# RWKV work given out anew over the 24 slots of a unit, with VectorE and ScalarE in emission order

## The chip, the cores and the metric

One core of a Trainium2 chip runs the kernel. The metric is the device time of one execution in microseconds (us). A core has a matrix engine (TensorE, PE in the profile, with its weight loads as PEld), VectorE (DVE), ScalarE (ACT), GpSimd (POOL) and SyncE (SP, which issues most DMAs).

## The reference, cut to what matters

A decoder layer on 1024 tokens of width 1024. After an RMSNorm, one projection feeds two branches whose outputs are concatenated, projected and normalised:

```python
p = einsum('bsd,dn->bsn', rms_norm(h, norm_w), w_in)     # 1024 x 8320 columns
y_rwkv = rwkv7_time_mix(p_shifted, gate, ...)            # 16 heads of 64
y_att = mixed_dilated_attention(p[..., ATT0:ATT_GATE0], p[..., ATT_GATE0:])
h = h + einsum('bsm,md->bsd', concatenate([y_rwkv, y_att]), w_out)
# inside rwkv7_time_mix, for each token t:
state = state * w_t + sa * b_t + v_t * k_t               # 64 x 64 per head
y_t = state @ r_t                                        # then group norm, bonus, gate
```

## The kernel before

All is float32. The RWKV recurrence is computed in chunks of 64 tokens. Two heads (a pair) and one half of the sequence (512 tokens, 8 chunks) make a *unit*; there are 16 units, `units[0..15]`. The loop over `p` from -2 to 15 in `rwkv` works on four units at once, in stages:

- `prepare` and `products` for unit p+2: norms of the keys (`norm`), decay rates (`decay`), running sums (`sums`), their exponentials, the removal keys and receptance, and 32 small matmuls per unit (`step`). `relayout` sends a triangular matrix through DRAM (`ld`) and `load` reads it back as `AB`.
- `late` and `invert` for unit p+1: transposes of keys and values, and a triangular inverse: 15 `column` steps on VectorE that read `AB` and write `UB`, then `back`, which sends `UB` through DRAM into `U`, then four matmul steps `m1` to `m4`.
- `chain` for unit p: the recurrence itself. Per chunk three steps (`first`, `second`, `third`); each is a few 128-column matmuls, then `spread`: one half of the result is copied by VectorE (zd, ud or Sd), the other by ScalarE, and the next step's matmul reads both. 8 chunks make 24 steps.
- `finish` for unit p-1: group norm (`norm`), transposes and gate (`store`), and the DMA to `mixd`.

Each pass over p has `NSLOT` = 24 slots. Slot s holds step s of the chain, and the other stages put their pieces into slots by number (constants `PREP`, `LATE`, `MS`, `FIN`, `COL0`, `BACK`, `LT`, `PROD`). After the pieces of a slot, `advance(4)` (in pass 13 `advance(2)`, before pass 0 `advance(5)`) emits *projection steps*: 512-column matmuls of the big input projection (`proj_steps`, L187), which have no tie to the chain. 24 of them make a half block; its last one is followed by `take` (one ScalarE and one VectorE pass over 128x512, `shift` or `gate`). A new weight block is fetched every 12 slots (`wload`: two ScalarE casts `wh` and two VectorE differences `wl`).

Emission order is not execution order. The framework's planner walks through the program once at build time with its own estimates of durations: each engine takes, among the instructions that are ready by that estimate, the one that was emitted first. Semaphores are added afterwards. On the chip each engine then follows that fixed order.

After the RWKV units come attention, which takes the remaining projection steps, and the output projection.

Of the kernel before, what the change touches and what calls it, by code (L numbers as in the profile page):

```python
# [20 lines left out]
HD = 64  # L21
# [3 lines left out]
C = 64  # L25
# [8 lines left out]
WARM = (4, 0)  # L34
V_AT = (-2, 3, -1)
COL0 = 0
COLN = 4
BACK = 9
LT = 12
MS = (16, 18, 20, 21)  # L40
LATE = (0, 3, 11, 10)
PREP = (2, 5, 6, 7, 8, 9, 10)
FIN = (1, 3, 7)
PROD = 10
# [9 lines left out]
class Kern:  # L54
# [237 lines left out]
    def rwkv(self, pairs=range(NPAIR), apairs=range(NPAIR)):  # L292
        nc = self.nc
        with ExitStack() as ctx:
# [49 lines left out]
            for p in range(-2, N):  # L344
                dA, dI, dC, dF = get(p + 2), get(p + 1), get(p), get(p - 1)
                ev = [[] for _ in range(NSLOT)]
                put = lambda steps: [ev[s].append(f) for s, f in steps]
                if dC:
                    put(enumerate(self.chain(dC, get(p + 1) if dC["h"] == 0 else None)))
                if dF:  # L350
                    put(self.finish(dF))
                if dI:
                    put(self.late(dI))
                    put(self.invert(dI, self.Us[(p + 1) % 2]))
                if dA:
                    lag = WARM[p + 2] if p < 0 else 0
                    put([(n + lag, f) for n, f in self.prepare(dA) + self.products(dA)])
                if get(p + 3) and get(p + 3)["h"] == 0:
                    ev[12].append(lambda d=get(p + 3): self.lora_w(d))
                elif get(p + 3):  # L360
                    get(p + 3)["lw"] = get(p + 2)["lw"]
                if p == -2:
                    px = self.prep_x(1, self.lng, tags, ba)
                    for s in range(4):
                        ev[s].append(lambda: [next(px, None) for _ in range(2)])
                    ev[4].append(lambda: [None for _ in px])
                n = 5 if p < 0 else 2 if dA is not None and get(p + 3) is None else 4
                for s in range(NSLOT):
                    for f in ev[s]:
                        f()  # L370
                    self.advance(n)
# [22 lines left out]
    def prepare(self, d):  # L394
# [8 lines left out]
        def decay():  # L403
# [6 lines left out]
            th = self.tmp("gt0", "th")  # L410
# [3 lines left out]
            lw = self.lw  # L414
# [4 lines left out]
        def sums(i):  # L419
# [6 lines left out]
            if i == 0:  # L426
                return
            I = d["I"]
            W = d["W"] = self.tmp("vr0", "W", L)
            S.activation(out=W, in_=I, func=AF.Exp, scale=-1.0)  # L430
            Ux = d["Ux"] = self.tmp("vr1", "Ux", L)
# [3 lines left out]
            S.copy(out=d["dec"][:, 1], in_=Ux[64:128, :, 0])  # L435

        def norm():
            sq = self.tmp("qr1", "sq")
            S.activation(out=sq, in_=d["ks"], func=AF.Square, scale=col(P_KK))
            sqt = self.ps_tr.tile([128, 4, 2, HD], F32, name="sqt", tag="tr")  # L440
            for b in range(4):
                nc.tensor.transpose(out=sqt[:, b].rearrange("p a b -> p (a b)"), in_=sq[:, b * 128:(b + 1) * 128],
                                    identity=self.ident)
            nq = self.mid.tile([128, 4, 2], F32, name="nq")
# [10 lines left out]
        def removal():  # L455
# [5 lines left out]
            V.scalar_tensor_tensor(out=b2, in0=c3(ta), scalar=1.0, in1=Ux[:, :, 1:C + 1], op0=ALU.add, op1=ALU.mult)  # L461
            V.scalar_tensor_tensor(out=b2, in0=c3(ks), scalar=col(P_KK), in1=b2, op0=ALU.mult, op1=ALU.mult)
            S.activation(out=ta, in_=ta, func=AF.Identity, scale=self.hka[:, pr:pr + 1], bias=self.oka[:, pr:pr + 1])
            V.tensor_tensor(out=ks, in0=ks, in1=ta, op=ALU.mult)
            V.tensor_tensor(out=BK[:, :, 64:128], in0=c3(ks), in1=Ux[:, :, 1:C + 1], op=ALU.mult)
# [10 lines left out]
        return list(zip(PREP, (norm, decay, lambda: sums(0), lambda: sums(1), removal, receptance, bonus_parts)))  # L476

    def late(self, d):
# [3 lines left out]
        pr = d["pr"]  # L482

        def values():
            vq = self.ps_tr.tile([128, 4, 2, HD], F32, name="vq", tag="tr")
            for b in range(4):
                nc.tensor.transpose(out=vq[:, b].rearrange("p a b -> p (a b)"), in_=d["vs"][:, b * 128:(b + 1) * 128],
                                    identity=self.ident)
            for par in range(2):
# [4 lines left out]
        def keys(c4):  # L494
            cs = slice(c4 * 4, c4 * 4 + 4)
            tq = self.ps_tr.tile([128, 4, 2, HD], F32, name="tq", tag="tr")
            for b in range(4):
                nc.tensor.transpose(out=tq[:, b].rearrange("p a b -> p (a b)"), in_=d["BK"][:, c4 * 4 + b],
                                    identity=self.ident)
            for e in range(2):  # L500
# [4 lines left out]
        def bonus():  # L505
            bq = self.ps_tr.tile([128, HALF], F32, name="bq", tag="tr")
            for i in range(2):
                nc.tensor.matmul(bq, lhsT=self.bdr, rhs=d["bs"][i], start=(i == 0), stop=(i == 1))
            d["bv"] = self.lng.tile([128, HALF], F32, name="bv", bufs=2)
            V.tensor_tensor(out=d["bv"], in0=bq, in1=d["vs"], op=ALU.mult)  # L510
        return list(zip(LATE, (lambda: keys(0), lambda: keys(1), values, bonus)))

    def products(self, d):
# [4 lines left out]
        def step(c4):  # L518
# [7 lines left out]
            for b in range(4):  # L526
                c = c4 * 4 + b
                for e in range(2):
                    nc.tensor.matmul(q[e][:, b], lhsT=BK[er[e], c], rhs=AR[er[e], c * 192 + 64:c * 192 + 192], start=True,  # L529
                                     stop=True)  # L530
            for e in (1, 0):
# [21 lines left out]
        steps = [(PROD + 2 * c4, lambda c4=c4: step(c4)) for c4 in range(2)]  # L553
        return steps + [(PROD + 5, relayout), (PROD + 5, load)]

    def invert(self, d, U):
# [33 lines left out]
        def m1():  # L590
# [3 lines left out]
            xq = self.ps_tr.tile([128, NC_, 16], F32, name="xq", tag="tr")  # L594
            for c in range(NC_):
                for g in range(4):
                    b = 32 * (g % 2)
                    nc.tensor.matmul(xq[hs(g), c], lhsT=t["LT"][rs(g), c, b:b + 16], rhs=U[rs(g), c, b + 16:b + 32], start=True,
                                     stop=True, skip_group_check=True)
            for g in range(4):  # L600
                S.copy(out=t["Xs"][hs(g), :, 0:16], in_=xq[hs(g)])
# [500 lines left out]
```

## Time and profile before

| what | value |
|---|---|
| median of three runs | 1561.51 us (1561.48 to 1563.06) |
| the profiled execution, its own time | 1562.53 us |
| its span in the trace | 1560.8 us |
| PE busy in the span | 1490.8 us (96%) |
| DVE busy | 1029.8 us (66%) |
| ACT busy | 891.8 us (57%) |
| mean granted TensorE clock | 0.997 of full |

The span is the trace from the first to the last instruction; the execution's own time has 1.7 us around it. The page's line of the clock shows full speed in all 40 slices. The chain of the first unit starts at about 118 us and that of the last ends at about 850 us. The chain of work that ended last is by engine PE 67%, DVE 18%, ACT 10%.

### The profile page before, as it was taken

To read this page: it belongs to the slowest core of one execution; us is meant where nothing else is said; L and a number is where in the kernel's file an instruction comes from. 1 tells how busy PE (TensorE), PEld (TensorE's weight loads), DVE (VectorE), ACT (ScalarE), POOL (GpSimd) and SP (SyncE) were. 2 spreads that over 40 slices of the span, in tenths; PEclk is the share of its full clock that TensorE was granted. 3 is DMA by queue.
4 is the path that set the end of the run, shared out by engine and by line. 5 is a ranking of instruction groups with operands and counts; after the bars stand their busy time and mean duration, and the time that the engine had idled before them with its cause. 6 is when DMAs were issued, how large, how long until landed. Compare 5 with 4: busy or idle time off the path is not lost.

```text
span 1560.8 us, 29095 instructions
## 1 busy us (share of the span) xinstructions
PE 1490.8 (96%) x10721; PEld 1211.8 (78%) x10721; DVE 1029.8 (66%) x2776; ACT 891.8 (57%) x2080; POOL 455.3 (29%) x563
## 2 busy tenths in 40 slices
PE   5999999999999999999999999999999999899997
PEld 4777777777777777777677788888888888787886
DVE  6867876777866768767644557666686676856144
ACT  6556666666666666665653556555565665645221
POOL 3122111121201212112111434333343344456442
PEclk9999999999999999999999999999999999999999
DMA  6221111111111111111111201111111111426452
GB/s 198 66 66 40 39 34 41 45 34 48 32 42 40 42 38 45 27 41 46 31 31 43 70 28 42 35 35 34 35 55 28 41 55 55 155 96 196 144 163 98
DMA packets 178829, 94.87 MB, mean 61 GB/s; under 512 B 58413, under 2 KB 164606, under 8 KB 178686
## 3 DMA queue, kind: packets, MB, share of 16 engines
q1 hardware_dynamic: 174942, 86.19, 19.4%
q10 hardware_dynamic: 3744, 6.82, 1.3%
q8 instruction: 84, 1.38, 0.4%
q14 instruction: 59, 0.48, 0.1%
HBM read 75.01 MB, written 17.83 MB: 59 GB/s over the span
## 4 chain that ended last, share of the span: by engine, by line
PE 67%; DVE 18%; ACT 10%; issue 3%; DMA 1%; POOL 1%; DVEq 0%; SPq 0%; POOLq 0%; ACTq 0%
PE pq L187 33%; PE oq L986 10%; PE T L645 4%; PE z L645 3%; PE o L932 3%; PE mp L859 2%; PE sp L892 2%; PE pa L529 2%; PE sp L912 1%; PE sp L911 1%; ACT zt L726 1%; DVE wl L179 1%; ACT MV L535 1%; PE x L621 1%; DVE I L424 1%
## 5 line engine op out<-in xcount | busy, mean ns | idle before, releaser
L187 PE MATMUL pq<-xh,wh 128*128 128x512 f32 x1040 | 428.9, 413 | 0.0
L187 PE MATMUL pq<-xl,wh 128*128 128x512 f32 x1040 | 416.4, 400 | 0.0
L187 PE MATMUL pq<-xh,wl 128*128 128x512 f32 x1040 | 294.8, 404 | 0.0
L187 PEld LDWEIGHTS pq<-xl,wh 128*128 128x128 f32 x1040 | 196.9, 189 | 32.0 <-DVE xl L166 0.2
L187 PEld LDWEIGHTS pq<-xh,wh 128*128 128x128 f32 x1040 | 196.5, 189 | 32.2 <-ACT xh L165 0.2
L187 PEld LDWEIGHTS pq<-xh,wl 128*128 128x128 f32 x1040 | 185.4, 189 | 31.9
L986 PE MATMUL oq<-ow,qr 128*128 128x512 f32 x512 | 161.9, 394 | 1.2 <-ACT ow L967 0.6
L920 POOL TENSOR_TENSOR pl<-p,ph 128x512 fp32r<-128x512 f32 (+2 forms) x96 | 102.2, 1071 | 202.5 <-ACT ph L919 182.3
L861 DVE CUSTOM_DVE_ANT_0 mp<-mp,maskq 128x512 f32<-128x512 f32 (+1 forms) x192 | 105.5, 570 | 67.6 <-PE mp L859 59.1
L915 ACT ACTIVATE p<-p 128x512 f32<-128x512 f32 (+2 forms) x144 | 64.6, 452 | 103.4 <-DVE p L914 102.5
L179 POOL TENSOR_TENSOR wl<-wraw,wh 128x512 fp32r<-128x512 f32 x64 | 85.2, 1351 | 110.5 <-ACT Sd L660 36.2
L981 POOL TENSOR_TENSOR vr<-kr,qr 128x512 fp32r<-128x512 f32 (+2 forms) x68 | 91.1, 1346 | 80.3 <-ACT qr L980 73.8
L986 PEld LDWEIGHTS oq<-ow,qr 128*128 128x128 f32 x512 | 95.9, 188 | 22.7 <-ACT ow L967 1.1
L986 PE MATMUL oq<-ow,vr 128*128 128x512 f32 x256 | 101.2, 395 | 2.0 <-POOL vr L981 2.0
L178 ACT CAST wh<-wraw 128x512 fp32r<-128x512 f32 x138 | 80.3, 618 | 39.2 <-PE pq L187 31.2
L980 ACT CAST qr<-kr 128x512 fp32r<-128x512 f32 (+2 forms) x68 | 40.1, 594 | 95.1 <-PE oq L986 49.8
L914 DVE TENSOR_TENSOR p<-sp,maskt 128x512 f32<-128x512 f32 (+2 forms) x144 | 65.2, 457 | 43.0 <-PE sp L912 41.5
L645 PEld LDWEIGHTS T<-ud,TU 128*128 128x128 f32 x256 | 40.8, 188 | 47.6 <-ACT ud L660 42.0
L660 ACT ACTIVATE Sd<-T,dec 64x64 f32<-64x64 f32 x120 | 36.9, 307 | 67.5 <-DVE Sd L659 66.2
L645 PE MATMUL T<-ud,TU 128*128 128x128 f32 x256 | 58.4, 310 | 16.8 <-ACT ud L660 15.6
L659 DVE TENSOR_SCALAR Sd<-T,dec 64x64 f32<-64x64 f32 x120 | 32.9, 274 | 60.4 <-PE T L645 58.2
L660 ACT ACTIVATE ud<-z,rn 64x64 f32<-64x64 f32 x128 | 39.3, 307 | 50.6 <-DVE ud L659 47.6
(236 smaller groups left out, 3173.5 us busy)
## 6 DMA issues: line engine op xcount, KB each, us to landing
wraw<-in_w_in_dram SPq DMA_DIRECT2D x138, 256.0 KB
kr<-mixd SPq DMA_DIRECT2D x60, 256.0 KB
oraw<-in_w_out_dram SPq DMA_DIRECT2D x16, 512.0 KB
xt<-in_x_dram SPq DMA_DIRECT2D x8, 512.0 KB
ld<-TU SPq DMA_DIRECT2D x32, 128.0 KB
mixd<-zt SPq DMA_DIRECT2D x16, 256.0 KB
mixd<-gt SPq DMA_DIRECT2D x16, 256.0 KB
xr<-in_x_dram ACTq DMA_DIRECT2D x16, 256.0 KB
```

The costliest lines, as they stand in the source:

```text
L178: nc.scalar.copy(out=wh[:, ks], in_=raw)
L179: eng.tensor_tensor(out=wl[:, ks], in0=raw, in1=wh[:, ks].bitcast(F32), op=ALU.subtract)
L187: return [lambda i=i, a=a, b=b: self.nc.tensor.matmul(q, lhsT=a, rhs=b, start=(i == 0), stop=(i == len(ops) - 1)) for i, (a, b) in enumera ...
L645: mm = lambda out, w, x, start, stop: nc.tensor.matmul(out, lhsT=w, rhs=f2(x), start=start, stop=stop, skip_group_check=True)
L660: S.activation(out=out[er[1], 1], in_=q[0:64, 64:128], func=AF.Copy, scale=scale[1])
L861: V.tensor_tensor_reduce(out=mp[:, :kn], in0=mp[:, :kn], in1=self.maskq[:, v0:v0 + kn], op0=ALU.add, op1=ALU.max, scale=1.0, scalar=-3e38, ...
L914: V.tensor_tensor(out=p[:, :qn], in0=sp[:, :qn], in1=self.maskt[:, u0:u0 + qn], op=ALU.add)
L915: S.activation(out=p[:, :qn], in_=p[:, :qn], func=AF.Exp)
L920: G.tensor_tensor(out=pl[:, :qn], in0=p[:, :qn], in1=ph[:, :qn].bitcast(F32), op=ALU.subtract)
L932: nc.tensor.matmul(oc, lhsT=v, rhs=w[:, :qn], start=(first and i == 0), stop=(last and i == len(prods) - 1), skip_group_check=True)
L981: nc.gpsimd.tensor_tensor(out=ml, in0=raw, in1=mh.bitcast(F32), op=ALU.subtract)
L986: nc.tensor.matmul(q, lhsT=m[:, i], rhs=v, start=(k == 0 and j == 0), stop=(k == 15 and j == 2))
```

## The change

Two things are changed, both inside `rwkv`. The loop over p now stands in a block in which the planner keeps VectorE and ScalarE in emission order; PE, GpSimd and SyncE are still placed by it. And the pieces are cut finer and put into other slots. Most pieces that had a matmul and the copy of its result in one slot now have the copy in the next slot.

| piece | slot before | slot after |
|---|---|---|
| keys transposes, halves 0 and 1 (PE / copies) | 0, 3 | 0 / 1, 2 / 3 |
| values (PE / copies), bonus (PE / product) | 11, 10 | 9 / 10, 11 / 12 |
| columns 0 to 14 | 0-3, four to a slot | 2,2,2,4,5,6,6,6,7,8,8,8,9,9,10 |
| back, lt | 9, 12 | 11, 12 |
| m1, m2, m3, m4 (PE) | 16, 18, 20, 21 | 16, 18, 21, 22 |
| their transposes and copies | same slots | 15; 17, 19 and 20, 22, 23 |
| key norms: square, PE, sums | 2 | 2, 4, 5 |
| decay: PE, tanh, log | 5 | 7, 8, 9 |
| running sums; W; Ux, dec, a | 6, 7; 7; 7 and 8 | 10, 11; 11; 12 |
| removal, receptance, bonus parts | 8, 9, 10 | 13-15, 16, 21 |
| products, two steps (PE / masks and copies) | 10, 12 | 17 / 18, 19 / 20 |
| relayout and load | 15 | 22 |
| finish: copy out, norm, store | 1, 3, 7 | 0; 1 to 4; 5 to 7 |
| lag of `prepare` in the first pass, `WARM` | 4 | 1 |

```diff
-            for p in range(-2, N):
+            with self.tc.manual_schedule(engines={mybir.EngineType.DVE, mybir.EngineType.Activation}):
+                for p in range(-2, N):
...
-        return list(zip(PREP, (norm, decay, lambda: sums(0), lambda: sums(1), removal, receptance, bonus_parts)))
+        return [(2, square), (4, squares), (5, norm), (7, decay), (8, rates), (9, logs), (10, lambda: sums(0)), (11, lambda: sums(1)),
+                (11, growth), (12, decrease), (13, removal), (14, removal2), (15, removal3), (16, receptance), (21, bonus_parts)]
...
-        return list(zip(LATE, (lambda: keys(0), lambda: keys(1), values, bonus)))
+        return [(0, lambda: keys(0)), (1, lambda: keys2(0)), (2, lambda: keys(1)), (3, lambda: keys2(1)), (9, values),
+                (10, values2), (11, bonus), (12, bonus2)]
...
-        steps = [(PROD + 2 * c4, lambda c4=c4: step(c4)) for c4 in range(2)]
-        return steps + [(PROD + 5, relayout), (PROD + 5, load)]
+        return [(17, lambda: step(0)), (18, lambda: step2(0)), (19, lambda: step(1)), (20, lambda: step2(1)), (22, relayout),
+                (22, load)]
...
+        return [(COLS[j], lambda j=j: column(j)) for j in range(15)] + [
+            (4, clear), (11, back), (12, lt), (15, m0), (16, m1), (17, m1c), (18, m2), (19, m2c), (20, m2t), (21, m3), (22, m3c),
+            (22, m4), (23, m4c)]
...
-        return list(zip(FIN, (lambda: self.heads_out(d, 1), norm, store)))
+        return [(0, lambda: self.heads_out(d, 1)), (1, norm), (2, squares), (3, root), (4, scale), (5, store), (6, turned), (7, gated)]
```

The new functions hold the same instructions as the old ones, cut apart. `root` (slot 3) is one reduction and the 13 dependent small operations of `rsqrt`; `decrease` (slot 12) is the exponential `Ux`, a small copy, and a full-width pass `a`, which now has a tile of its own (tag gt0) in place of overwriting `ta`. `lora_w` (four small ScalarE casts, in every second pass) stays in slot 12, as the last piece of the slot. The steps of the chain and the four projection steps per slot are unchanged.

## Rows read from the trace of the kernel before

**Rows 1.** Busy time by stretch: stretch, length, PE, PEld, DVE, ACT, POOL, clock, DMA.

```profile
161.50:777.00 615.50, 590.79 (x5723) 465.90 (x5722) 448.00 (x1391) 394.15 (x1034) 113.77 (x207) 1.00 0.16 39
816.09:850.17 34.08, 33.80 (x191) 26.43 (x189) 12.71 (x44) 14.42 (x40) 5.21 (x5) 1.00 0.13 40
27.00:118.50 91.50, 85.66 (x605) 68.05 (x604) 66.19 (x139) 53.48 (x108) 16.94 (x33) 1.00 0.27 75
```

**Rows 2.** Waits of weight loads, 161.5 to 777 us: total us, times, longest.

```profile
PEld T L645 <- ACT ud L660: 33.7, 47, 1.4
PEld z L645 <- ACT zd L657: 16.1, 27, 1.9
PEld z L645 <- ACT Sd L660: 12.3, 46, 0.8
```

**Rows 3.** Timeline of PE in one unit: start, duration, engine, line, operation, tiles.

```profile
448.27 0.40 PE L645 MATMUL z<-Sd,AR 128*66 128x128 f32 x2
...
451.99 0.60 PE L442 MATMUL sqt<-ident,sq 128*128 128x128 f32 x4
452.34 0.48 PE L187 MATMUL pq<-xh,wh 128*128 128x512 f32 x1
...
458.86 1.09 PE L187 MATMUL pq<-xh,wl 128*128 128x512 f32 x4
459.78 0.38 PE L645 MATMUL z<-Sd,AR 128*66 128x128 f32 x2
...
469.76 1.16 PE L529 MATMUL pa<-AR,BK 64*128 64x128 f32 x16
...
481.22 0.69 PE L598 MATMUL xq<-U,LT 32*16 32x16 f32 x64
...
495.56 0.38 PE L645 MATMUL z<-Sd,AR 128*66 128x128 f32 x2
```

**Rows 4.** Timeline of VectorE in the same unit.

```profile
456.03 0.17 DVE L77 TENSOR_TENSOR rs_w<-gr 128x8 f32<-128x8 f32 x1
456.23 0.17 DVE L78 TENSOR_TENSOR rs_w<-rs_w,rs_x 128x8 f32<-128x8 f32 x1
...
466.54 0.73 DVE L462 SCALAR_TENSOR_TENSOR BK<-ks,prm,BK 128x512 f32<-128x512 f32 x1
467.20 0.21 DVE L656 COPY zd<-z 64x64 f32<-64x64 f32 x1
467.38 0.69 DVE L464 TENSOR_TENSOR ks<-ks,ta 128x512 f32<-128x512 f32 x1
```

**Rows 5.** Timeline of ScalarE in the same unit.

```profile
461.51 0.30 ACT L390 CAST lhi<-lraw 64x128 fp32r<-64x128 f32 x1
461.83 0.64 ACT L430 ACTIVATE W<-I 128x520 f32<-128x520 f32 x1
...
463.14 0.74 ACT L726 COPY zt<-yq 64x256 f32<-64x256 f32 x2
463.90 0.31 ACT L660 ACTIVATE ud<-z,rn 64x64 f32<-64x64 f32 x1
...
465.01 0.82 ACT L463 ACTIVATE ta<-ta,hk 128x512 f32<-128x512 f32 x1
...
493.02 1.15 ACT L178 CAST wh<-wraw 128x512 fp32r<-128x512 f32 x2 [0.37 <-PE pq L187]
```

**Rows 6.** Projection steps alone, by unit: unit 12 and unit 13.

```profile
685.10:732.50 47.40, 28.48 (x96) 16.39 (x96) 1.00 0.16 39
732.50:778.00 45.50, 19.89 (x59) 10.52 (x59) 0.96 0.16 40
```

**Rows 7.** DMA issues on SyncE's queue in the same unit: start, duration, count.

```profile
457.69 3.64 SPq L583 DMA_DIRECT2D U<-ud  x8
...
478.11 1.31 SPq L544 DMA_DIRECT2D ld<-TU  x2
481.94 1.81 SPq L550 DMA_DIRECT2D AB<-ld  x4
```

More of the change, by code (lines that the diff above doesn't have):

```diff
@@ L343, in rwkv @@
             self.lora_w(units[0])
-            for p in range(-2, N):
[L345 to L371, printed above, removed]
@@ new lines, in rwkv @@
+            with self.tc.manual_schedule(engines={mybir.EngineType.DVE, mybir.EngineType.Activation}):
+                for p in range(-2, N):
+                    dA, dI, dC, dF = get(p + 2), get(p + 1), get(p), get(p - 1)
+                    ev = [[] for _ in range(NSLOT)]
+                    put = lambda steps: [ev[s].append(f) for s, f in steps]
+                    if dC:
+                        put(enumerate(self.chain(dC, get(p + 1) if dC["h"] == 0 else None)))
+                    if dF:
+                        put(self.finish(dF))
+                    if dI:
+                        put(self.late(dI))
+                        put(self.invert(dI, self.Us[(p + 1) % 2]))
+                    if dA:
+                        lag = WARM[p + 2] if p < 0 else 0
+                        put([(n + lag, f) for n, f in self.prepare(dA) + self.products(dA)])
+                    if get(p + 3) and get(p + 3)["h"] == 0:
+                        ev[12].append(lambda d=get(p + 3): self.lora_w(d))
+                    elif get(p + 3):
+                        get(p + 3)["lw"] = get(p + 2)["lw"]
+                    if p == -2:
+                        px = self.prep_x(1, self.lng, tags, ba)
+                        for s in range(4):
+                            ev[s].append(lambda: [next(px, None) for _ in range(2)])
+                        ev[4].append(lambda: [None for _ in px])
+                    n = 5 if p < 0 else 2 if dA is not None and get(p + 3) is None else 4
+                    for s in range(NSLOT):
+                        for f in ev[s]:
+                            f()
+                        self.advance(n)
@@ L435, in sums, with square, squares @@
             S.copy(out=d["dec"][:, 1], in_=Ux[64:128, :, 0])
[L437 to L439 removed]
+            t["a"] = self.tmp("gt0", "a")
+            S.activation(out=t["a"], in_=ta, func=AF.Identity, scale=self.hka[:, pr:pr + 1], bias=self.oka[:, pr:pr + 1])
+        t = {}
+        def square():
+            t["sq"] = self.tmp("qr1", "sq")
+            S.activation(out=t["sq"], in_=d["ks"], func=AF.Square, scale=col(P_KK))
+        def squares():
+            sq = t["sq"]
             sqt = self.ps_tr.tile([128, 4, 2, HD], F32, name="sqt", tag="tr")
@@ L599, in m1, with m1c @@
                                      stop=True, skip_group_check=True)
+        def m1c():
             for g in range(4):
-                S.copy(out=t["Xs"][hs(g), :, 0:16], in_=xq[hs(g)])
+                S.copy(out=t["Xs"][hs(g), :, 0:16], in_=t["xq"][hs(g)])
         def m2():
-            dq = self.ps_tr.tile([128, NC_, 16], F32, name="dq", tag="tr")
+            dq = t["dq"] = self.ps_tr.tile([128, NC_, 16], F32, name="dq", tag="tr")
             for c in range(NC_):
@@ L622, in m3, with m3c @@
                                      stop=True, skip_group_check=True)
+        def m3c():
             for e in range(2):
-                S.copy(out=t["Xs"][hi[e]], in_=x2[hi[e]])
+                S.copy(out=t["Xs"][hi[e]], in_=t["x2"][hi[e]])
         def m4():
@@ L631, in m4, with m4c @@
                                      skip_group_check=True)
+        def m4c():
             for e in range(2):
-                S.copy(out=U[lo[e], 0:NC_, 32:64], in_=x2[lo[e]])
-        return [(COL0 + j // COLN, lambda j=j: column(j)) for j in range(15)] + [(BACK - 5, clear), (BACK, back), (LT, lt)] + list(zip(MS, (m1, m2, m3, m4)))
+                S.copy(out=U[lo[e], 0:NC_, 32:64], in_=t["x2"][lo[e]])
+        return [(COLS[j], lambda j=j: column(j)) for j in range(15)] + [
+            (4, clear), (11, back), (12, lt), (15, m0), (16, m1), (17, m1c), (18, m2), (19, m2c), (20, m2t), (21, m3), (22, m3c),
+            (22, m4), (23, m4c)]
     def chain(self, d, nxt):
```

83 lines of the change are left out of this document (55 added, 28 removed).

## The prediction, made before the changed kernel ran

> **What bounds the kernel now.** I read the busy time by stretch first, then the waits of the weight loads, then the timelines of one unit. The change touches only the RWKV stage, so only its units count: 13 of them, passes 0 to 12, follow each other in a fixed period. One period goes from 448.27 to 495.56, which is 47.3 us [rows 3], or 615.5/13 = 47.35 us, 1.97 us per slot [rows 1].
>
> PE is busy 590.8 of 615.5 us there [rows 1], which looks full. But matmuls overlap in the pipeline, so I work out what PE needs. Four projection steps in a row take 459.78 - 458.86 = 0.92 us, 0.23 each [rows 3]. The last unit holds the chain, its 96 projection steps and one group of four transposes, and little else: 34.08 us for 23 slots [rows 1]. A group of transposes costs 452.34 - 451.99 = 0.36 [rows 3], so a bare slot is (34.08 - 0.36)/23 = 1.47 us, and 24 of them 35.2. On top a full unit has five groups of transposes (1.8), the four decay matmuls (0.92, taken as 1.0 for the change of tile), the two of the bonus (0.5), m1 to m4 at 0.65 each (the row says 0.69 with its overlap; 2.6) and two product steps at 1.1 (2.2) [rows 3]. The sum is 43.3 us. So about 4.0 us per unit are waits that the matmul row hides, 52 us in 13 units. The waits of the weight loads say where: (33.7 + 16.1 + 12.3)/13 = 4.8 us per unit before a chain matmul, until ScalarE's half of ud, zd or Sd is there [rows 2] (part of it while the matmul before still runs). Those halves are late because other work stands before them: ud at 463.90 follows a pair of zt copies without a pause [rows 5].
>
> The Trainium skill, Perfetto Trace Analysis, section Identifying the Most-Contended Engine, says that matmul busy share is no measure of headroom and the share of weight loads is. By it the headroom here would be 1 - 465.9/615.5 = 24%, or 11.5 us per unit, and the best end near 1412 us. The bare slot of the last unit doesn't bear that out, and I keep 4.0.
>
> **The change part by part.** No instruction is removed; `a` gets its own tile. What changes is the load of each slot. With VectorE and ScalarE in emission order, the chain's copy of slot s+1 stands behind everything that slot s gave that engine. So a slot lasts as long as the longest of three sums: PE's, VectorE's, ScalarE's. Prices, from start to start: VectorE 0.66 for a fused pass over 128x512 and 0.61 for a plain one (0.69 less the 0.07 of overlap that the fused one shows), 0.2 for a small dependent operation, so 0.4 for a column, 0.2 for the chain's copy [rows 4]; scans as plain passes. ScalarE: 0.38 for a quarter copy (0.74 for two), 0.65 for a full-width pass, 0.82 for `a`, 0.57 for a weight cast, 0.32 for a small cast or copy, 0.33 for the chain's copy [rows 5]. Takes and weight blocks are put where emission puts them: the end of slots 5, 11, 17, 23, and slots 0 and 12. The unit's sums come to 35.8 for VectorE and 33.5 for ScalarE; measured are 448.0/13 = 34.5 and 394.2/13 = 30.3 [rows 1]. I therefore scale by 0.96 and 0.91. Slots 0 to 23 after the change:
>
> PE: 1.8 1.5 1.8 1.5 1.8 1.8 1.5 2.5 1.5 1.8 1.5 2.0 1.5 1.5 1.5 1.5 2.1 2.6 2.1 2.6 1.5 2.1 2.1 1.5 (43.3).
> VectorE: 1.4 1.6 1.3 3.3 1.2 2.8 1.3 1.8 1.3 1.5 1.2 1.4 2.5 1.5 1.4 1.4 0.8 0.8 1.4 0.2 1.9 0.8 0.8 0.8.
> ScalarE: 2.0 1.7 1.5 1.7 0.3 1.1 1.7 0.3 1.5 0.3 1.7 1.5 2.9 (4.0 in every second pass) 0.3 0.3 0.3 0.3 2.7 1.5 1.5 1.5 0.9 1.0 1.6.
>
> Most slots now lie under PE's sum: that is the gain, and the burst that products, masks and removal made is gone. Four slots stick out: slot 3 (`root`, a reduction and 13 dependent operations) by 1.8, slot 12 (`decrease`, `lora_w` and the weight casts) by 1.4 or 2.6, slot 5 (columns, key norm, take) by 0.9, slot 20 by 0.5; slots 0, 1, 6, 10, 17 and 23 by 0.2 or less each. Together 5.8 or 6.9, 6.35 on average. If PE kept four steps in every slot, a unit would last 43.3 + 6.35 = 49.7 us.
>
> The cover is that the planner lets PE run projection steps of later slots while the chain is held; then later slots have fewer and PE makes up. That it does so is seen where PE had little: in unit 13, where 48 steps are emitted, 59 ran [rows 6], so 11 ahead, 2.5 us. The bounds are none covered (49.7) and all covered (43.3; VectorE and ScalarE alone would allow 41.7, the sum of the longer of the two). The planner goes by estimates and sees a lump only as far as these are right. I take four fifths of the three largest (1.8 + 2.0 + 0.9 = 4.7, so 3.8 covered) and nothing of the rest: 43.3 + 2.55 = 45.85.
>
> The Trainium skill, Perfetto Trace Analysis, section Per-engine timelines, says that the queues of VectorE, ScalarE and GpSimd are strictly first in, first out. By it alone no chain copy can pass a lump, and the unit would be the 49.7 of the uncovered case. The ud behind the zt copies agrees [rows 5]; what it leaves open is whether PE has something else to do.
>
> Two waits on DMAs are now in VectorE's order. `relayout` ends in slot 22 and column 0 stands in slot 2: 1.3 + 1.6 + 2.0 + 1.7 + 0.2 = 6.8 us. The trip takes 481.94 - 478.11 = 3.8 to the second hop, 1.8 to issue that, and about 2.5 to land, by what the first hop needs after its 1.3 of issues [rows 7]: an estimated 8.1. Column 0 would be 1.3 late, and everything of VectorE behind it, the chain's zd of slot 3 first. Slot 2 has 0.5 to spare, so 0.8 at most and nothing at least; I take 0.3, since slots 22 and 23 grow when PE catches up there. The other trip (last column in slot 10, `m0` in slot 15) has 9.5 us against 0.65 (half of the two ld issues) + 2.5 + 3.64 + 2.5 = 9.3 [rows 7], and I take nothing. A unit is then 46.15, a gain of 1.2, in 13 units 15.6 us.
>
> Outside: units 13 to 15 have no or less preparation but keep `root`; two lumps of 1.8, partly covered, +1.5. The first two passes (27 to 118.5 us) have PE busy 85.7 of 91.5 [rows 1]; up to 5.8 could be won, and VectorE's wait for AB there (only some 4 us of slots lie between) could lose as much. I take 0. Attention and output are as before. The sum: 1562.5 - 15.6 + 1.5 = 1548.4 us for the profiled execution; the median of the runs lies 1.0 lower, so **1547 us**.
>
> **The rivals.**
> *All lumps covered.* PE never lacks steps and a unit is 43.3 to 44.3: 40 to 53 us less, 1510 to 1523. For it: 11 steps ahead in unit 13 is more than any lump needs. Against it: in the period now, 4 us of waits stay although the planner could have covered them.
> *Slower: the lumps stay in the chain.* The planner underrates `root` and slot 12 and PE stands with the chain. It decides when less than 2.65 of the 6.35 us (6.35 + 0.3 - 4.0) are covered, some 11 steps per unit; with none covered a unit is 50.0, +34 us, 1597. For it: the waits of today are just such unforeseen ones.
> *Slower: the trip through DRAM.* If SyncE's queue holds another load in front, AB comes 3 us later than reckoned, VectorE stands in slot 2, and a unit is 2.0 to 2.5 longer than forecast: 1575 to 1580. It decides from 1.2 us of extra delay on.
> *No change.* The planner already went nearly by emission order, and lumps won and lost cancel: 47.1 to 47.6 per unit, 1558 to 1565.
>
> **How the numbers follow.** Forecast (1523 to 1558) 0.43, all covered 0.12, no change 0.11, lumps stay 0.20, trip 0.14. So faster 0.55, within 0.2% (3 us, about what a measurement of this kernel can tell) 0.11, slower 0.34. The likeliest case gives 1547. The range leaves out the lower half of the covered case (0.06) and the upper part of the slower ones (about 0.12): 1517 to 1584.
>
> **What would show it.** The period between two chain starts: 46 if right, 43 to 44 or 48 to 50 for the rivals. Slots 16 to 22 near PE's sum, slots 3 and 12 the longest. Projection steps ahead of emission by more than ten after slots 3 and 12. Weight loads waiting less than 62 us for the chain's copies. It is wrong if the chain waits at slot 3 with no steps run meanwhile, or if VectorE's idle time before column 0 ends on a DMA for more than 1.5 us per unit.

## The result and the profile after

| | before | after |
|---|---|---|
| median | 1561.49 us (1561.05 to 1563.06, 4 runs) | 1653.62 us (1651.77 to 1655.49, 4 runs) |
| span in the trace | 1560.8 | 1650.0 |
| mean granted TensorE clock | 0.997 | 0.979 |

The ratio is 1.0588, 95% interval 1.057 to 1.0606. The kernel became 92 us slower; 1547 was forecast, with 1517 to 1584 as the range.

The page of the changed kernel: its span, busy time by engine, and the granted clock in 40 slices.

```profile
span 1650.0 us, 29033 instructions
PE 1520.5 (92%) x10721; PEld 1222.1 (74%) x10721; DVE 1044.8 (63%) x2776; ACT 892.9 (54%) x2080; POOL 430.7 (26%) x563
PEclk9999999999999999999989999999999999999999
```

Where the time lies is read from the chain's starts. The first matmul of the chain's second unit starts at 164.0 us before and at 179.2 after, that of the fourteenth at 732.5 and 812.1, and the chain's last matmuls start at 850.2 and 937.9. So the lead-in and the first unit take 15.2 us more, units 1 to 12 64.4 (47.37 and 52.74 each), the last three 8.1, and the rest of the kernel 1.5: 89.2, the difference of the spans.

The windows of units 1 to 12, first in the kernel before and then in the changed one (length, then busy time of PE, PEld, DVE, ACT, POOL, then the granted clock):

```profile
164.00:732.50 568.50, 548.89 (x5306) 433.87 (x5305) 416.77 (x1304) 364.31 (x955) 103.06 (x193) 1.00 0.16 40
```
```profile
179.20:812.10 632.90, 566.86 (x5307) 439.70 (x5305) 427.87 (x1302) 365.21 (x954) 82.15 (x192) 0.98 0.14 35
```

The engines do the same work, but PE's idle time is 66.0 us in place of 19.6: 46.4 of the 64.4 us. The other 18.0 are busy time of PE that has grown, about half of it by the clock (below). What PE's matmuls waited for there, in the changed kernel (total, times, longest):

```profile
PE pq L179 <- DVE rs L216: 19.8, 12, 2.0
PE pq L179 <- DVE gt L251: 16.3, 12, 1.7
PE T L694 <- ACT ud L709: 14.3, 24, 1.3
PE z L694 <- ACT zd L706: 12.2, 13, 1.0
```

The first two rows are new. PE has run as far ahead as it can: the next projection block needs one of the two PSUM banks of `pq`, and the bank is free only when VectorE has done `rs` or `gt`, the last pass of a *take* (ScalarE reads the block's result into `shtmp` or `tg`, then VectorE reads it once more). PE's order is fixed, so the chain's matmuls stand behind the step that waits. VectorE's waits in the same window:

```profile
DVE wl L171 <- ACT wh L170: 43.7, 24, 2.6
DVE vs L216 <- ACT shtmp L213: 27.5, 12, 2.6
DVE ks L216 <- issue: 17.1, 6, 2.9
DVE rs L216 <- ACT shtmp L213: 15.5, 12, 1.6
DVE ks L216 <- ACT shtmp L213: 13.5, 6, 2.3
DVE gt L251 <- ACT tg L249: 13.0, 12, 1.4
```

Five of these rows, 113 us or 9.4 a unit, are the second half of a pair whose first half is ScalarE's: a take, or a weight block (`wh`, then `wl`). The row with "issue" stands at a take too, with no releaser that the profile shows. Before, the largest row at a take or weight block was 3.7 us. Rows picked from the timeline at slots 11 to 13 of a unit show how that reaches the chain:

```profile
521.86 0.58 ACT L249 ACTIVATE tg<-pq 128x512 f32<-128x512 f32 x1
522.47 0.69 DVE L251 SCALAR_TENSOR_TENSOR gt<-tg,pq 128x512 f32<-128x512 f32 x1 [1.44 <-ACT tg L249]
523.07 0.21 DVE L705 COPY zd<-z 64x64 f32<-64x64 f32 x1
523.21 0.50 PE L179 MATMUL pq<-xh,wh 128*128 128x512 f32 x1 [1.02 <-DVE gt L251]
523.32 0.20 ACT L706 COPY zd<-z 64x64 f32<-64x64 f32 x1 [0.88 <-DVE zd L705]
523.55 0.64 ACT L434 ACTIVATE Ux<-I 128x520 f32<-128x520 f32 x1
...
524.22 0.20 ACT L437 COPY dec<-Ux 64x8 f32<-64x8 f32 x1
...
524.25 0.19 POOL L436 COPY dec<-Ux 64x8 f32<-64x8 f32 x1 [2.25 <-ACT Ux L434]
...
526.42 1.14 ACT L170 CAST wh<-wraw 128x512 fp32r<-128x512 f32 x2
527.07 1.30 DVE L171 TENSOR_TENSOR wl<-wraw,wh 128x512 fp32r<-128x512 f32 x2 [2.58 <-ACT wh L170]
528.29 0.27 DVE L708 TENSOR_SCALAR ud<-z,rn 64x64 f32<-64x64 f32 x1
```

After slot 12 ScalarE works from 523.55 to 527.6, VectorE waits 2.58 for its first cast and does `wl`, and only then comes the chain's `ud`, at 528.29, 5.2 us after `zd`. The two engines' work stands one behind the other. Also, ScalarE's copy of the chain begins only after VectorE's has ended (`zd` at 523.07 and 523.32), and so it is with all 376 pairs of these copies in the trace. Both read the same partitions of one PSUM tile. That both write one tile is not the reason: two engines write `dec` at once, at 524.22 and 524.25. So work in front of VectorE's copy delays ScalarE's as well. The Trainium skill, PSUM — Partial Sum Buffer, section Terms, counts it as an error when two engines access the same bank and quadrant at once, reads against reads included; the order of these rows agrees.

The last part is PE's clock. First the five windows around a bank stop, then three whole units of the changed kernel:

```profile
299.00:301.00 2.00, 1.41 (x11) 1.11 (x10) 1.55 (x7) 0.37 (x3) 0.00 (x0) 1.00 0.00 0
301.00:303.00 2.00, 0.84 (x2) 0.70 (x3) 1.49 (x6) 1.08 (x4) 0.00 (x0) 0.81 0.00 0
303.00:305.00 2.00, 2.00 (x7) 1.57 (x6) 1.69 (x6) 1.27 (x4) 0.00 (x0) 0.50 0.00 0
305.00:307.00 2.00, 2.00 (x11) 1.69 (x10) 1.52 (x6) 0.33 (x2) 0.00 (x0) 0.84 0.26 100
307.00:309.00 2.00, 2.00 (x13) 1.69 (x13) 1.36 (x8) 1.45 (x3) 0.00 (x0) 1.00 0.08 31
...
285.30:338.40 53.10, 47.53 (x447) 37.15 (x443) 35.64 (x108) 30.72 (x81) 7.16 (x16) 0.97 0.14 36
495.50:547.50 52.00, 46.37 (x447) 35.84 (x443) 35.37 (x108) 30.73 (x81) 7.16 (x16) 1.00 0.15 37
705.30:760.30 55.00, 49.40 (x451) 38.46 (x444) 34.96 (x108) 30.73 (x81) 6.99 (x16) 0.94 0.13 34
```

After this stop the clock goes from 2.4 to 1.2 GHz (0.50) and comes back. A unit without such a fall lasts 52.0 us, one with a short fall 53.1, one with a long one 55.0. The kernel before shows 1.00 over its twelve units. Five of the changed kernel's twelve show 1.00 as well and last 51.8 to 52.4 us, so by an estimate from these only some 9 to 10 of the 64.4 us are the clock's.

### The profile page after: what moved, and what is told of

The parts are those of the page before. It is cut to its first block, busy times and chain, and to the rows that moved or that the text cites. A ratio compares the mean times of both kernels' runs of the same rounds, so it can differ in the third digit from the quotient of the medians.

```text
span 1650.0 us, 29033 instructions
## 1 busy us (share of the span) xinstructions
PE 1520.5 (92%) x10721; PEld 1222.1 (74%) x10721; DVE 1044.8 (63%) x2776; ACT 892.9 (54%) x2080; POOL 430.7 (26%) x563
## 4 chain that ended last, share of the span: by engine, by line
PE 55%; DVE 21%; ACT 13%; issue 5%; DMA 3%; POOL 2%; SPq 0%; DVEq 0%; POOLq 0%; ACTq 0%
PE pq L179 27%; PE oq L1049 9%; PE o L995 3%; PE T L694 2%; PE z L694 2%; PE mp L922 2%; PE pa L560 2%; PE sp L955 2%; ACT shtmp L213 2%; DVE wl L171 1%; ACT Vd L514 1%; DMA wraw<-in_w_in_dram 1%; DVE UB L607 1%; PE sp L975 1%; PE sp L974 1%
## 5 line engine op out<-in xcount | busy, mean ns | idle before, releaser
L179 PE MATMUL pq<-xh,wh 128*128 128x512 f32 x1040 | 433.6, 417 | 45.3 <-DVE rs L216 22.4
L179 PE MATMUL pq<-xl,wh 128*128 128x512 f32 x1040 | 424.3, 408 | 0.0
L179 PEld LDWEIGHTS pq<-xh,wh 128*128 128x128 f32 x1040 | 200.1, 193 | 85.6 <-DVE rs L216 25.6
L179 PEld LDWEIGHTS pq<-xl,wh 128*128 128x128 f32 x1040 | 200.5, 193 | 31.7 <-DVE xl L158 0.2
L171 POOL TENSOR_TENSOR wl<-wraw,wh 128x512 fp32r<-128x512 f32 x64 | 85.5, 1355 | 113.7 <-ACT wh L170 71.6
L1043 ACT CAST qr<-kr 128x512 fp32r<-128x512 f32 (+2 forms) x68 | 40.2, 594 | 96.3 <-PE oq L1049 49.7
L171 DVE TENSOR_TENSOR wl<-wraw,wh 128x512 fp32r<-128x512 f32 x74 | 48.8, 699 | 50.8 <-ACT wh L170 50.7
```

The costliest lines, as they stand in the source:

```text
L171: eng.tensor_tensor(out=wl[:, ks], in0=raw, in1=wh[:, ks].bitcast(F32), op=ALU.subtract)
L179: return [lambda i=i, a=a, b=b: self.nc.tensor.matmul(q, lhsT=a, rhs=b, start=(i == 0), stop=(i == len(ops) - 1)) for i, (a, b) in enumera ...
```

## The experiments

All are made from the changed kernel (K) unless said otherwise; times are medians. The table gathers units 1 to 12 of each run: length of a unit and PE's idle time in it (from the windows, divided by 12), and the granted clock.

| run | time, us | unit | PE idle | clock |
|---|---|---|---|---|
| before | 1561.5 | 47.4 | 1.6 | 1.00 |
| the change (K) | 1653.6 | 52.7 | 5.5 | 0.98 |
| e1_slots_only | 1555.0 | 47.4 | 1.8 | 1.00 |
| e2_order_only | 1785.6 | 63.2 | 11.4 | 0.88 |
| e3_order_vector | 1603.9 | 49.9 | 1.8 | 0.99 |
| e4_order_scalar | 1589.9 | 49.4 | 3.4 | 1.00 |
| m1_takes_apart | 1666.8 | 53.9 | 5.8 | 0.94 |
| m2_weights_apart | 1663.8 | 54.2 | 5.2 | 0.95 |
| m3_both_apart | 1641.0 | 51.6 | 4.0 | 0.97 |
| m4_order_from_first_chain | 1636.6 | 53.3 | 5.4 | 0.97 |
| f1_takes_free | 1603.1 | 51.3 | 3.3 | 0.97 |
| f3_free_and_apart | 1602.1 | 51.0 | 3.1 | 0.97 |
| k1_takes_free_weights_in_order | 1647.8 | 53.0 | 4.7 | 0.95 |
| k2_k1_order_from_first_chain | 1634.1 | 52.9 | 4.2 | 0.95 |
| k3_weights_free_takes_in_order | 1679.3 | 55.9 | 5.7 | 0.92 |
| p1_pe_in_order | 1795.1 | 63.0 | 12.8 | 0.89 |
| p2_both_apart_pe_in_order | 1672.3 | 53.5 | 7.5 | 0.97 |
| s1_slots_only_lag0 | 1559.4 | 47.3 | 1.8 | 1.00 |
| b1_slots_apart_planner | 1546.5 | 46.5 | 1.9 | 1.00 |
| b2_before_apart | 1555.1 | 47.3 | 1.4 | 1.00 |

### Slots or order, and which engine

```diff
-with self.tc.manual_schedule(engines={DVE, Activation}):
+if True:                                              # e1
+with self.tc.manual_schedule(engines={DVE}):          # e3
+with self.tc.manual_schedule(engines={Activation}):   # e4
```
e2 puts the loop of the kernel before, with its old slots, into the block of the change.

> The new slots, without the order of emission: VectorE and ScalarE are ordered by the planner as before. Theory A (pairs): the loss of 92 us is made by the order. In it a take of a projection (ScalarE shtmp or tg, then VectorE) and a weight block (ScalarE wh, then VectorE wl) stand as a whole in front of the chain's next copy, so that the slot lasts ScalarE's part plus VectorE's part, and PE stops when both banks of the projection wait for such a take. With the planner free to move them the loss goes: 1550 to 1575 us, the waits of wl and of the takes on ScalarE (74 us over both engines in the profile of the change) fall below 25. Theory B (slots): the places themselves are bad, 13 units of 52.7 us stay, 1630 to 1650. Theory C (start): the first unit is 15 us late because of WARM (1, 0) and the columns' new slots; then about 15 us of the loss stay here, 1570 to 1580.

> The slots of the kernel before, with VectorE and ScalarE in the order of emission. Theory A (pairs): slower than the change itself, 1700 to 1800 us, because here each matmul of a step and its copy stand in one slot too, so that the chain's next copy stands behind PE as well; a unit lasts 56 us or more. Theory B (slots): the order costs little, 1565 to 1600.

> The change with VectorE alone in the order of emission; ScalarE by the planner. Theory A (pairs): ScalarE may now do shtmp, tg and wh early, so that most of VectorE's waits on them go (94 us of wl, vs, ks, rs and gt on ScalarE in the profile of the change): 1580 to 1620 us. Theory B (slots): no change, 1640 to 1655.

> The change with ScalarE alone in the order of emission; VectorE by the planner. Theory A (pairs): VectorE may put the chain's copy before a wl or a take that is not ready, so the pairs no longer stand in front of the chain; what stays is ScalarE's own lump in front of its copy (4.0 us after slot 12): 1565 to 1610 us. Theory B (slots): no change, 1640 to 1655.

e1: 1555.0 us, 0.9952 of before (0.9935 to 0.9969). The new slots cost nothing; the order makes the whole loss and 7 us more. e2: 1785.6, within what A gave; the old slots with the order are worse by 132 us than the new ones. e3 and e4 lie within A as well: the order on VectorE alone costs 49 us against e1, on ScalarE alone 35, on both 99. B is out. In e3 VectorE's waits for ScalarE's halves are gone, but the chain now comes to column 0 earlier than its transfer, which the change itself never showed:

```profile
DVE TB L605 <- DMA AB<-ld: 33.4, 12, 3.6
```

C looks to the start. e1's second unit begins at 158.2 us, 5.8 before that of the kernel before and 21 before that of K, so the late start too is the order's, not WARM's.

### The two halves apart

In `stream`, VectorE's half of a take, and in `wload` the two `wl`, are put on a list and emitted some projection steps later.

```diff
+TAKE_LAG, WL_LAG = 2, (5, 9)
-                take(h, q)
+                rest = take(h, q)                       # m1, m3: ScalarE's half only
+                later.append([TAKE_LAG, rest])
...
-            eng.tensor_tensor(out=wl[:, ks], in0=raw, in1=..., op=ALU.subtract)
+            later.append([WL_LAG[i], low])              # m2, m3: low() is that pass
```
In m4 the two lead-in passes stay with the planner:

```diff
-            with self.tc.manual_schedule(engines={DVE, Activation}):
-                for p in range(-2, N):
+                for p in range(-2, N):
+                    if p == 0:
+                        order.enter_context(self.tc.manual_schedule(engines={DVE, Activation}))
```

> The change, with VectorE's half of each take (the shift's or the gate's last pass) emitted two projection steps after ScalarE's half, so that it stands behind the chain's copies of the next slot and not in front of them. Theory A (pairs): in the profile of the change VectorE waits 84 us for shtmp and tg in units 1 to 12, 7 us a unit, part of it on the chain's way; that goes, and the chain gets back 2.5 to 3.5 us a unit of 13: 1608 to 1622 us. Theory D (lumps alone: what costs is how long the work in front of the copy lasts, not who waits for whom): the same work stands a slot later, so no change, 1645 to 1655. Theory E (banks: PE stops because both banks of the projection wait for a late take): the take frees its bank still later, so PE's stops on rs and gt (41 us in units 1 to 12) grow and the time is 1655 to 1670.

> The change, with the two wl passes of a weight block on VectorE emitted five and nine projection steps after the casts wh on ScalarE, so one and two slots later, behind the chain's copies there. Theory A (pairs): VectorE waits 44 us for wh in units 1 to 12, 3.7 us every unit, most of it after slot 12 where the casts stand behind four lhi casts; slot 12 gives back 1.5 to 2.5 us and slot 0 about 1: 1610 to 1630 us. Theory D (lumps alone): 1645 to 1655.

> Both of the runs before together: takes and wl behind the chain's copies. Theory A (pairs): a unit falls from 52.7 to 47.5 to 49 us, so 1583 to 1602 us; it does not reach the 1555 of the slots without the order, since the first unit's late start stays (21 us against that run) and since column 0 then comes before its transfer has landed, as in the run with VectorE alone in order, where it waited 2.7 us a unit. Theory D (lumps alone): 1640 to 1655.

> The change, with the order of emission only from the unit on in which the chain starts; the two units of lead-in are ordered by the planner. Theory A says that the start is the same kind of loss as the units: the second unit begins 21 us later in the change than in the run with the slots alone (179.2 and 158.2 us), and that comes back, 13 to 20 us: 1633 to 1641. The rival: the lead-in is set by PE, which was busy 94% of it before, and the late second unit comes from the first unit's own order: at most 5 us come back, 1648 to 1655.

m1: 1666.8, in E's range; m2: 1663.8, in none; both slower than K. m3: 1641.0, 13 us faster, but 39 short of A's upper end and at the edge of D's range. A's mechanism was right only in the place: the waits at the halves that were moved went (in m2, `wl` on `wh` fell to 7 us; in m1, where it was not moved, it rose to 57), the time did not. Three things took the gain. First the clock: in m2 ten of the twelve units ran into a fall, unit 1 did not (the windows show units 1 and 7):

```profile
177.40:229.10 51.70, 46.72 (x452) 35.92 (x445) 35.37 (x108) 30.78 (x81) 7.45 (x16) 1.00 0.15 37
502.20:556.90 54.70, 49.74 (x452) 38.59 (x445) 34.93 (x108) 30.77 (x81) 7.26 (x16) 0.94 0.14 35
```

With the same instructions in the same order and the same idle time of PE (5.0 us), that is 3.0 us a unit. Without a fall m2's unit is as long as K's (51.7 against 52.0). Second, other stops: in m1 PE's stops for a bank fell from 36.1 to 22.2 us, not up as E had it, and in their place the inverse came to its transfer too early:

```profile
PE xq L649 <- DMA U<-ud: 18.7, 19, 2.6
```

Third, in m3 PE itself. The chain's `zd` was ready at 493.6 us, and its matmul came at 498.56, since PE's fixed order had 21 projection steps in front (this window shows only those steps; DVE's next chain copy waits for PE):

```profile
493.60:498.50 4.90, 4.60 (x21) 3.47 (x19) 1.00 0.19 54
```
```profile
498.98 0.28 DVE L726 TENSOR_SCALAR ud<-z,rn 64x64 f32<-64x64 f32 x1 [2.59 <-PE z L712]
```

The steps of the chain show where the wait went. Each goes from a matmul to VectorE's copy, to ScalarE's copy, to the next matmul. The table sums this over the 24 steps of unit 6 from the starts and ends in the timelines (us). It counts from the last copy of the unit before, so its sums are some 1 us longer than the unit. The granted clock of the unit is 1.00 in all four.

| from ... to | before | e1 | K | m3 |
|---|---|---|---|---|
| end of the matmul to VectorE's copy | 8.4 | 7.4 | 17.3 | 5.8 |
| end of VectorE's copy to ScalarE's copy | 5.4 | 7.1 | 3.0 | 7.8 |
| end of ScalarE's copy to the next matmul | 12.1 | 11.8 | 10.1 | 15.3 |
| the matmuls and copies themselves | 22.5 | 22.3 | 22.5 | 22.5 |
| all | 48.4 | 48.6 | 52.9 | 51.4 |

```profile
443.73:495.48 51.75, 46.37 (x446) 35.68 (x441) 35.74 (x109) 30.13 (x78) 6.56 (x16) 1.00 0.14 35
```
```profile
435.81:485.99 50.18, 46.28 (x447) 35.81 (x442) 35.78 (x109) 30.17 (x78) 6.57 (x16) 1.00 0.14 37
```

These windows are unit 6 of K and of m3. K's loss stands in front of VectorE's copies: some 9 us more than before. With the halves apart that wait is gone, below its old level, and most of what it gave back is lost again in front of PE, 5.2 us more than in K, and of ScalarE, 4.8 more. Against e1, which has the same slots, m3's remaining 2.8 us lie with PE (3.5 more). Of PE's stops for a bank m3 has 5.0 us left in units 1 to 12.

m4: 1636.6, 17 us back, as A gave it: the second unit starts at 161.0 in place of 179.2. The lead-in's order costs by itself.

### PE in order

```diff
-with self.tc.manual_schedule(engines={DVE, Activation}):
+with self.tc.manual_schedule(engines={DVE, Activation, PE}):   # p1 from K, p2 from m3
```

> The change with PE in the order of emission as well, so that exactly four projection steps stand between two chain steps; the planner's order of PE lets it run up to 22 steps ahead. Theory G (what PE runs ahead covers part of the lumps): each lump now stands in the chain, no bank stop is left, a unit of 54 to 58 us: 1670 to 1730. Theory H (PE's planned order is itself wrong by what the chip does, and the chain's matmuls stand behind projection steps): each unit at most the 49.7 to 50.0 us that the slots' sums give, 1600 to 1625.

> Takes and wl apart from their ScalarE halves (as in m3_both_apart, 1641 us) and PE in the order of emission. In m3 a chain matmul that was ready stood behind 20 projection steps, 4.6 us, after slot 3. Theory H (PE's planned order is what took the gain of m3): 1585 to 1612 us, below m3 by 30 or more. Theory G (running ahead is needed): 1640 to 1690.

p1: 1795.1, even above G. H is out: running ahead gives back 10.3 us a unit (63.0 against 52.7), what it does to the clock included (0.89 and 0.98). p1 is also the case of my table, four steps in every slot, for which the sums gave 49.7. In its twelve units VectorE's longest waits at takes and weight blocks are (that with "issue" has no releaser in the profile):

```profile
DVE wl L171 <- ACT wh L170: 43.7, 24, 2.6
DVE ks L216 <- issue: 36.8, 6, 6.1
...
DVE vs L216 <- ACT shtmp L213: 29.9, 12, 3.0
DVE rs L216 <- ACT shtmp L213: 22.3, 12, 2.9
DVE gt L251 <- ACT tg L249: 19.2, 12, 2.5
```

p2 lies within G: 1672.3, slower than m3. PE's planned order took part of m3's gain (the table above), but PE in plain order takes more. Against p1 the halves apart give 123 us: where nothing runs ahead, the pairs are worth 9.5 us a unit, the clock included (0.89 and 0.97).

### Takes and weights out of the order

f1 draws the order over the work of the slots alone; the takes and casts that come with the projection are left to the planner. k1 puts the weight blocks back, k3 the takes; k2 is k1 with the order from p = 0. f3 is f1 with the later emission of m3.

```diff
                     for s in range(NSLOT):
                         for f in ev[s]:
-                            f()
+                            self.ordered(f, (DVE, Activation))      # edge from each instruction to the next
                         self.advance(n)
...
+            wn = self.ordered(lambda: load(jobs[i + 1]), ...)        # k1, k2
+                self.ordered(lambda: take(h, q), ...)                # k3
```

> The change, with the order of emission drawn for the work of the slots alone: what comes with the projection (its takes and the casts of its weights, on both engines) is left to the planner. Theory F (banks): in units 1 to 12 PE stands idle for 66.0 us in the change and for 19.6 before, and 36 us of it are stops of a projection step on rs and gt, which free a bank late because the order holds them back. With the takes free these stops and the waits of VectorE on shtmp, tg and wh go, and the clock stays up: a unit of 48.5 to 50 us, 1583 to 1608 us, most of what is left being the first unit. Rival (the slots' own order is the loss, and the takes only show it): 1635 us or more, with PE's idle time on z and T in place of the stops.

> As f1_takes_free (1603 us), but the casts of the weight blocks (wh, wl) are back in the order of emission; only the takes are left to the planner. If the takes in order are what holds the banks (theory F), the stops on rs and gt stay away and the time is 1585 to 1615: the planner's misplaced wl, which in f1 waited up to 4.6 us for its buffer in every second unit, goes, and the wait of wl on wh after slot 12, about 2 us a unit, comes back. If it was the weight blocks in order that cost (theory W), this run is back at 1635 to 1655.

> The counterpart: takes in the order of emission as in the change, the weight blocks left to the planner. Theory F: PE's stops on rs and gt stay at about 36 us in units 1 to 12 and the clock falls after them: 1630 to 1660. Theory W: 1600 to 1615, as f1.

> k1 with the order only from the unit on in which the chain starts. The second unit began at 179.2 us in the change, at 165.2 in f1 (takes free) and at 161.0 in m4 (lead-in free). If the late start is the takes' too, this run is only 2 to 6 us faster than k1; if the lead-in's order costs by itself, 13 to 18 us faster, as m4 against the change.

> f1 (takes and weight blocks left to the planner, 1603 us) with the VectorE halves emitted later as in m3 and b1. Every second unit of f1 lasted 53.0 us in place of 48.7 to 48.9 because the planner put wl before its buffer was free (28 us of wl waiting for PE). If that is all that keeps f1 up, all units are at 48.7: 1575 to 1585. If the slots' own order holds the rest whatever the wl does, 1598 to 1606. Either way what stays over b1 (1546) is the price of the slots' own order with takes and weights out of it.

f1: 1603.1, as F gave it, 51 us back; the bank stops fell from 36.1 us to 1.2. k1 (1647.8) lies where W had it, but k3 (1679.3) in neither range, so neither theory holds for both. With the takes alone free the stops on `rs` and `gt` are gone and 45 us of the 51 are not there; with the weights alone free it is 26 us slower than K. In both runs the clock fell further (0.95, 0.92). So F as the single cause has fallen. How much either pair costs in order these runs don't tell: in k3 the freed `wl` waited 44.7 us for its buffer, a wait that K doesn't have. These five also force the order in another way than K, by edges from instruction to instruction, and no run has both pairs in order in that way; so their differences against K hold that change too.

In f1 a new wait appears: the planner put the freed `wl` at a place where its buffer was still being read by PE, in front of the chain's copy. The timeline of DVE in unit 8, one of six units of 53.0 to 53.9 us:

```profile
528.87 0.17 DVE L622 TENSOR_TENSOR UB<-UB,TB 64x15 f32<-64x15 f32 x1
533.31 0.69 DVE L172 TENSOR_TENSOR wl<-wraw,wh 128x512 fp32r<-128x512 f32 x1 [4.27 <-PE pq L180]
```

f3 was to remove that and did not: 1602.1, with the same wait and the same units of 53.0. What the order of the slots' own work costs without it was not measured; 48 us lie between f1 and e1, and this wait is in them. k2 is 13.7 us faster than k1, with the second unit at 159.7 in place of 173.4: the lead-in's order costs by itself, as in m4.

### Versions in the planner's order

b1 is e1 and b2 the kernel before, each with m3's edits in `stream` and `wload`; s1 is e1 with one constant changed:

```diff
-WARM = (1, 0)
+WARM = (0, 0)
```

> The slots alone with the planner's order, as in e1 (1555 us), with the lead-in's first unit placed one slot earlier (0 in place of 1). The 7 us that e1 gained over the kernel before are in its start (chain 4.8 us earlier, second unit 5.8 us) and none in its units, 47.4 us as before. If the place of the first unit is what gives it, another 1 to 2 us come: 1552 to 1554. If it is the new slots of the steps, no change: 1554 to 1557.

> The slots with the planner's order (e1, 1555 us) and takes and wl emitted later as in m3. The planner places by its own times, so if the place of emission matters only where it is the order, no change: 1553 to 1558. If the planner breaks ties by the place of emission, the chain's copies come first and a unit falls under 47: 1540 to 1550.

> The kernel before, with the VectorE halves of takes and weight blocks emitted later as in b1, nothing else. Between e1 and b1 a unit fell from 47.4 to 46.5 us, 8.5 us in all. If that comes from the place of emission alone, the kernel before gets the same: 1550 to 1556. If it needs the new slots, no change: 1559 to 1565.

s1: 1559.4, neither of the two: slower, with the chain's start back at 118.5 us (e1 113.7). The first unit's place decides most of e1's gain, but one slot earlier is worse. b1: 1546.5, 0.9889 of before (0.9873 to 0.9906), the fastest version, in the range of the second reading; its unit is 46.5:

```profile
161.50:719.80 558.30, 535.22 (x5307) 424.71 (x5306) 399.15 (x1302) 369.23 (x955) 93.31 (x192) 1.00 0.16 40
```

b2: 1555.1, in the range of the first reading: the later emission alone gives the kernel before 7 us, but not where b1 has them: its twelve units give 0.9 us (47.4 to 47.3), its second unit starts 4.0 us earlier. b1's units give 10.2 us against before. That gain needs the new slots and the later emission together; the new slots alone (e1) give none in the units either.

## Why the prediction was wrong

**The bound now.** Right: PE and its waits bound the units. The five versions in the planner's order keep PE's idle time at 1.4 to 1.9 us a unit, and K has 5.5. Idle time alone doesn't tell it: e3 has 1.8 too and a unit of 49.9, with 48.0 us of PE's busy time where the kernel before has 45.7. One slip in the reading: the window from 161.5 to 777 us holds units 1 to 13, not passes 0 to 12, and unit 13 lasted 43.0 us; the period of 47.3 and the 4.0 us of waits stay as they were.

**"A slot lasts as long as the longest of three sums."** This step failed. It takes the engines as independent within a slot. But takes and weight blocks are pairs, ScalarE then VectorE, and stood whole in front of the chain's copies; and the chain's ScalarE copy starts behind VectorE's. There the sums add up: in unit 6 the chain's copies wait 17.3 us for VectorE, 8.4 before, and 5.8 with the halves apart (m3). The skill's rule that I weighed (the Trainium skill, Perfetto Trace Analysis, section Per-engine timelines: VectorE's, ScalarE's and GpSimd's queues are strictly first in, first out) spoke against the change, and the waits of `wl`, `ks`, `vs`, `rs` and `gt` agree with it. I used it one engine at a time. The uncovered unit that I put at 49.7 was 63.0 (p1). Of these 13.3 us, 6.9 are at most the clock (755.6 x 0.11/12). The other 6.4 and more I put to waits like the five rows of p1 above, 12.7 us a unit, part of them on the chain's way. p2, with the halves apart, is at 53.5; its units at a clock of 1.00, all in passes without `lora_w`, last 51.3 to 51.4, and the sums gave 49.1 (43.3 + 5.8) for such a pass.

**The cover of 3.8 us.** Its mechanism was right: PE runs ahead after slots 3 and 12, and by more than ten. The windows count the projection steps from a unit's start to the matmul of slot 4, where 16 are emitted, and to that of slot 14, where 56 are:

```profile
495.50:507.05 11.55, 8.86 (x32) 5.65 (x32) 1.00 0.31 76
...
495.50:529.30 33.80, 22.34 (x78) 13.45 (x78) 1.00 0.17 41
```

16 and 22 ahead. All that PE runs ahead is worth 10.3 us a unit (p1, the clock included), more than I took. But it has an end that I did not look for: two banks, and a take that frees one only at its place in VectorE's order. At that end PE stops with the chain's matmuls behind it, 3.0 us a unit. The Trainium skill, Perfetto Trace Analysis, section Optimization Strategy, says that the same gap repeating on the engine that should be full can mean too little SBUF or PSUM for the next tile; the two rows of 12 stops agree.

**Lumps.** Slot 12's work makes the longest interval of the chain, as the table had it (5.2 us from `zd` to `ud` in the timeline), but as the sum of ScalarE's 4.0 and VectorE's `wl`. At `root` PE had steps to run: 21 were done by the matmul of slot 3 and 32 by that of slot 4.

**The DMA trips.** K's rows show no wait for AB; its chain was slower. In e3 VectorE waited 2.8 us a unit for it, near the 2.0 to 2.5 of my rival. In m1 PE waited 1.6 a unit for U. A rival that is hidden may come out when another wait goes.

**Outside.** The lead-in was taken as 0 with 5 us either way and cost 15.2 at the second unit; m4 gave 18.2 there back. Which part of its order costs that stays open. Units 13 to 15 were taken as +1.5 and cost 8.1.

**The rivals.** "The lumps stay in the chain", at 1597, had the right sign and the wrong mechanism and size: its worst unit of 50.0 was below the 52.7 that came although PE ran ahead. The clock was in none of the cases.

**The signs.** Neither of the two signs of being wrong came: at slot 3 PE ran steps, and no DMA ended VectorE's idle time at column 0. A sign of being right came beside a loss: weight loads waited 60.4 us for the chain's copies in units 1 to 13 (179.2 to 859.8 us), less than 62. That row doesn't count the chain's matmuls behind a stopped projection step, nor the wait in front of VectorE's copy.

What stays open is how the loss divides between the pairs' wait in front of the chain and the bank stops (m3 takes away both), why PE's fixed order costs more in m3 than in e1, and what decides whether the clock falls.

## What to carry to other kernels

Before an engine is put in a fixed order, list the instructions there whose input comes from another engine at the same place in the order; add those times in series, not as a maximum, and emit the second half after what must not wait. Count the buffers that limit how far the engine that covers the lumps can run ahead, and see which instruction frees one. Where a planner orders, emission later is still a lever: the second halves behind the critical copies gave 1.1% together with the new slots (b1), and no order by force was needed. And see where a wait goes when it is taken away: in m3 it went from VectorE to PE's fixed order.

## What the runs showed of the hardware

I had not expected the clock. Waits of PE can cost twice: after PE had stood idle for some of its time its granted clock could fall to 0.50, and in m2 a unit of the same instructions then took 54.7 us in place of 51.7. These windows of K lie at the same place in two units, 495.5 and 705.3:

```profile
531.00:535.00 4.00, 2.67 (x25) 1.99 (x25) 3.08 (x7) 1.60 (x6) 0.00 (x0) 1.00 0.04 12
535.00:539.00 4.00, 3.01 (x89) 2.46 (x85) 2.10 (x4) 2.40 (x7) 0.51 (x3) 1.00 0.01 4
539.00:543.00 4.00, 4.00 (x36) 3.39 (x36) 1.88 (x5) 2.27 (x8) 1.43 (x3) 1.00 0.00 0
741.00:745.00 4.00, 2.67 (x26) 2.08 (x26) 2.95 (x7) 1.72 (x6) 0.00 (x0) 1.00 0.00 0
745.00:749.00 4.00, 3.01 (x88) 2.37 (x84) 2.22 (x5) 2.33 (x7) 0.51 (x3) 1.00 0.02 4
749.00:753.00 4.00, 4.00 (x21) 3.78 (x22) 0.69 (x4) 2.08 (x7) 1.32 (x2) 0.55 0.00 0
```

PE was busy for 2.67 and 3.01 of 4 us in both; only in the second the clock fell to 0.55 in the next 4 us, and PE did 21 matmuls there in place of 36. What decides it the rows don't say. A stop for a bank is not needed: f1 has 1.2 us of them in all, and its five units of 48.7 to 49.5 us show a clock of 0.93. The Trainium skill, TensorE: Matmul & The Clock Gate, section A second HAM failure mode: psum-queue depth-cycling, tells of a kernel whose PE stood idle briefly between groups of matmuls as it cycled through PSUM, and whose clock went up and down; K's windows from 299 to 309 us agree.
